# A kernel of one decoder layer: the left operands of the first feed-forward's deferred products are stored whole and split when they are fetched

## The chip, the cores and the metric

The kernel runs on one core of one Trainium2 chip. The core has engines with instruction queues of their own, each worked off in order: TensorE (PE; its weight loads are listed as PEld), VectorE (DVE), ScalarE (ACT), GpSimd (POOL), and SyncE (SP), which here issues all DMAs. The metric is the device time of one execution in microseconds (us); less is better.

## The reference

One layer of a sequence of 1024 tokens with width 1024: a half-step feed-forward, a mixer (a short convolution beside a state-space model), a second half-step feed-forward and a last norm. The change touches the two feed-forwards only.

```python
def swiglu(h, w_gate, w_up, w_down):
    return (jax.nn.silu(h @ w_gate) * (h @ w_up)) @ w_down
...
h = modulate(rms_norm(x, ffn1_norm[l]), sh1, sc1)
x = x + 0.5 * g1[:, None, :] * swiglu(h, ffn1_w_gate[l], ffn1_w_up[l], ffn1_w_down[l])
```

D_FF is 2816. All is float32.

## The kernel before

**Products.** A float32 product is made of three matmuls. Each operand is split into a high part (ScalarE rounds it to `fp32r`, a CAST) and a low part (VectorE subtracts the high part from the whole); then high x high, high x low and low x high are added in PSUM (`mm3`, line 333). A split operand of 128 x 512 is a tile of two halves, 512 KB; the whole is 256 KB.

**Groups.** The 22 column tiles of D_FF are taken in 11 groups of two. With the two halves of the tokens a group's activations are a 2 x 2 block matrix: A11, A12, A21, A22, each 128 x 512. For groups 4 to 10 of the first feed-forward (`fa4` to `fa10`) and 1 to 10 of the second (`fb1` to `fb10`) the gate and up products are made with seven block products in place of eight (`seven`, line 575): TensorE fills the PSUM banks A, B, C, D, E of the gate side, then of the up side (`fa8gC`: group 8, gate side, bank C), and VectorE adds them up in `t`, `u` tiles (`fa8gt`, `fa8gu`, `fa8ut`, `fa8uu`). Groups 0 to 3 of the first feed-forward use plain products (`gate_up`, line 1157).

**Deferred down products.** The down products of groups 1 to 8 are made later, in two chunks of four groups, again with seven block products, so their left operands are seven sums and blocks: A11, S1, S2, S3, A12, A22, S4 (`keep_sums`, `keep_last`, lines 490 to 501). Those of groups 0, 9 and 10 stay plain (`LAST`, line 39) and need the four A blocks. `keep` (line 482) splits an operand as soon as it is there, in a tile of the pool `movA`, and SyncE stores the 512 KB of both parts in DRAM. `fetch` (line 650) reads them back when a left operand of the chunk ahead has been used up.

**Passes.** `down7` (line 655) works a chunk in two passes, each over a quarter of the output columns from both halves. A pass has seven steps in the order A11, S2, A12, S3, S1, A22, S4 (`SECOND`, line 573), each 8 x 3 matmuls into banks A, B, C of two outputs (`fad_0A`: bank A of output 0). So there are passes 1 and 2 (chunk 0) and 3 and 4 (chunk 1). In a chunk's second pass each step's operand is given up, and SyncE fetches the next chunk's into the tiles that become free: `then(left)`. The operands of chunk 0 are fetched in the same way on the up side of group 10. The names of fetched tiles are `fa1lA`, `fa1lS` and so on: group 1, operand A.. or S... Behind pass 4 the last parts follow (`fald`, groups 0, 9, 10).

**Weights.** They come in `raw` tiles of 1 MB (two buffers), and one step of a pass needs one split weight tile `w` in a ring of three; `Weights.pump` (line 182) splits the next when a ring slot becomes free. A pass needs two raw tiles (`in_ds`), seven weight tiles with two halves, one from each raw tile; GpSimd makes four of the sums from the raw tiles (lines 164 to 175). The two raw tiles of the next pass can be loaded when the last weight tile of this one has been split.

**What sets the order.** The program is written in the order above, and side work (the state-space matrices, the modulation vectors `wm`) is let in by a count of matmuls (`Clock`). A scheduler then puts each engine's instructions in a row of its own, by the time at which it believes each can start and by the tiles that are free; in that row they run in order, so an instruction that waits holds all behind it.

Of the kernel before, what the change touches and what calls it, by code (L numbers as in the profile page):

```python
# [13 lines left out]
F32 = mybir.dt.float32  # L14
# [3 lines left out]
ALU = mybir.AluOpType  # L18
# [3 lines left out]
P = 128  # L22
D = 1024
S = 1024
HALF = 512
# [206 lines left out]
def hymba_layer(ctx: ExitStack, tc, x_d, wm1_d, wmod_d, gu1_d, gs1_d, ds1_d, wl1_d, win_d, wout_d, glu_d, gu2_d, gs2_d, wd2_d, ds2_d, wl2_d, cols_d, cond_d, lam_d, bc_d, out_d):  # L232
# [257 lines left out]
    def keep_sums(kept, a11, a21, a22, name):  # L490

        V.tensor_tensor(out=a22[:], in0=a21[:], in1=a22[:], op=ALU.add)
        keep(kept, "S1", a22, name)
        V.tensor_tensor(out=a21[:], in0=a11[:], in1=a21[:], op=ALU.subtract)
        keep(kept, "S3", a21, name)
        V.tensor_tensor(out=a22[:], in0=a22[:], in1=a11[:], op=ALU.subtract)
        keep(kept, "S2", a22, name)

    def keep_last(kept, a12, s2, name):
        V.tensor_tensor(out=a12[:], in0=a12[:], in1=s2[:], op=ALU.subtract)  # L500
        keep(kept, "S4", a12, name)

    def gu_keep(fi, h, pg, pu, afs, kept, name):
        t = t2k(f"{name}{fi}_{h}")
        A.activation(t[:], pg[:], AF.Silu)
        V.tensor_tensor(out=t[:], in0=t[:], in1=pu[:], op=ALU.mult)
        keep(kept, f"A{h + 1}{fi + 1}", t, name)
        afs[fi, h] = t
        if len(afs) == 4 and "S1" in kept:
            keep_sums(kept, afs[0, 0], afs[0, 1], afs[1, 1], name)  # L510
            keep_last(kept, afs[1, 0], afs[1, 1], name)
# [63 lines left out]
    def seven(name, between, place=1, kept=None, then=None):  # L575
# [4 lines left out]
        for side in "gu":  # L580
# [5 lines left out]
            def out(h, fi, t):  # L586
                nm = f"{name}_{fi}_{h}"
                if side == "g":
                    A.activation(t[:], t[:], AF.Silu)
                    gate_[h, fi] = t  # L590
                else:
                    V.tensor_tensor(out=t[:], in0=t[:], in1=gate_[h, fi][:], op=ALU.mult)
                    if kept is None:
                        a_tiles[fi, h] = split_act(t[:], nm + "a")
                    else:
                        keep(kept, f"A{h + 1}{fi + 1}", t, name)

            for n, (left, b) in enumerate(SEVEN):
# [26 lines left out]
                elif n == 4:  # L625
                    t = gate_[0, 0]
                    V.tensor_tensor(out=t[:], in0=t[:], in1=bank["A"][:], op=ALU.mult)
                    if kept is None:
# [1038 lines left out]
```

## Time and profile before

| what | us |
|---|---|
| median of 3 runs (1743.46 to 1748.77) | 1745.43 |
| the profiled execution, whole | 1741.48 |
| its span, first to last instruction | 1739.7 |
| groups of the first feed-forward | 50 to 501 |
| passes 1 to 4 | 501, 539, 582, 620, to 660 |
| last parts and the next norm | 660 to 730 |
| mixer | 730 to 1050 |
| second feed-forward: groups, passes | 1150 to 1510, 1510 to 1700 |

How to read the rows that follow: in a view by stage, each engine's busy time stands with its count of instructions, then the granted clock of TensorE (1.00 is full), the busy share of the DMA engines and their rate. In a view of time, a row has its start, its length, engine, line, operation and tiles, and in brackets the idle time of that engine ahead of it with what ended it. Nearly all instructions carry line 107, that of the helper which issues them, so one goes by the tiles' names; numbers of buffers are left out of them. In a view of waits, the three numbers are the total, the count and the longest. In a view of DMA issues, the last number is the median time from issue to landing.

### The profile page before, as it was taken

The page shows a single profiled execution, that of the slowest core. Times are in us where ns is not written, and L with a number is a line of the kernel's source. Part 1 is how long each engine was busy: PE and PEld are TensorE (multiplying, and loading weights), DVE is VectorE, ACT ScalarE, POOL GpSimd, SP SyncE. Part 2 cuts the span into 40 slices and gives each one's busy share as a digit, 9 for nine tenths or more (in the row PEclk, how much of TensorE's full clock was granted, in tenths as well). Part 3 has the DMA queues.
Part 4 walks back from the last instruction along what each step waited for, and adds up shares of the span by engine and source line. Part 5 has one row for each costly group of instructions (what it writes and reads, how often), then busy time and mean ns, then how long its engine had stood idle before and what let it go on. Part 6 is the DMA issues. An engine that isn't in the chain of part 4 may idle for free.

```text
span 1739.7 us, 20839 instructions
## 1 busy us (share of the span) xinstructions
PE 1672.0 (96%) x7532; PEld 1375.3 (79%) x7532; DVE 1291.1 (74%) x2261; ACT 573.3 (33%) x944; POOL 352.8 (20%) x241
## 2 busy tenths in 40 slices
PE   4999999999999999999999999999999999999996
PEld 3788888787887878887877778778888888888886
DVE  7999999998656787644657977967776666576656
ACT  4233334344332222331114424424444433322221
POOL 0000132222422221100000021123223323333211
PEclk9999999999999999999999999999999999999998
DMA  8245644555787877234654450114344334659212
GB/s 322 84 145 197 220 158 167 179 201 173 286 307 275 321 259 270 73 86 147 209 152 152 134 181 25 49 49 157 144 175 166 133 138 152 249 235 379 104 49 97
DMA packets 101338, 304.56 MB, mean 175 GB/s; under 512 B 19313, under 2 KB 34929, under 8 KB 90098
## 3 DMA queue, kind: packets, MB, share of 16 engines
q1 hardware_dynamic: 101234, 303.22, 49.0%
q8 instruction: 59, 0.97, 0.2%
q14 instruction: 45, 0.37, 0.1%
HBM read 212.47 MB, written 86.51 MB: 172 GB/s over the span
## 4 chain that ended last, share of the span: by engine, by line
PE 64%; DVE 8%; DMA 3%; issue 1%; ACT 0%; POOL 0%; SPq 0%; DVEq 0%; ACTq 0%; POOLq 0%
PE wo L107 4%; PE fald L107 3%; PE fb10d L107 2%; PE u L107 2%; PE fbd_1B L107 2%; PE fbd_0B L107 2%; PE fad_1B L107 2%; DVE w L107 2%; PE fad_0B L107 2%; PE b L107 2%; DMA swz<-si 1%; DVE x L107 1%; PE fb0g L107 1%; PE fbd_1C L107 1%; PE fbd_0C L107 1%; PE fbd_1A L107 1%
## 5 line engine op out<-in xcount | busy, mean ns | idle before, releaser
L107 ACT CAST w<-raw 128x512 fp32r<-128x512 f32 (+1 forms) x358 | 235.9, 689 | 459.1 <-issue 70.1
L107 DVE TENSOR_TENSOR w<-raw,w 128x512 fp32r<-128x512 f32 (+1 forms) x358 | 300.9, 860 | 100.8 <-ACT w L107 99.9
L164 POOL TENSOR_TENSOR sums<-raw 128x512 f32<-128x512 f32 x50 | 73.8, 1476 | 452.9 <-DMA raw<-in_gs 271.0
L173 POOL TENSOR_TENSOR raw<-sums,raw 128x512 f32<-128x512 f32 x50 | 78.4, 1568 | 367.3 <-DVE w L107 353.7
L107 DVE CUSTOM_DVE_ANT_0 wm<-wm,cact 128x1024 f32<-128x1024 f32 x56 | 77.7, 1396 | 22.6 <-DMA wm<-in_wmod 22.6
L175 POOL TENSOR_TENSOR raw<-raw 128x512 f32<-128x512 f32 x50 | 77.1, 1542 | 79.1 <-DVE w L107 79.1
L165 POOL TENSOR_TENSOR raw<-raw 128x512 f32<-128x512 f32 x50 | 77.3, 1547 | 3.1
L366 POOL TENSOR_TENSOR n3aq<-n3aq,n3aq 128x512 f32<-128x512 f32 x5 | 7.4, 1474 | 279.1 <-ACT n3aq L107 278.9
L107 DVE TENSOR_TENSOR w<-sums,w 128x512 fp32r<-128x512 f32 x50 | 56.7, 1147 | 5.4 <-ACT w L107 4.8
L107 PE MATMUL p<-h,w 128*128 128x512 f32 x192 | 49.6, 421 | 8.1 <-DVE h L107 5.3
L107 PEld LDWEIGHTS p<-h,w 128*128 128x128 f32 x192 | 39.1, 205 | 18.6 <-DVE h L107 6.5
L107 PE MATMUL wo<-oa,w 128*128 128x512 f32 x192 | 45.6, 392 | 2.1 <-ACT w L107 1.4
L107 PE MATMUL v<-h,w 128*128 128x512 f32 x192 | 46.8, 395 | 0.0
L107 PE MATMUL c<-h,w 128*128 128x512 f32 x192 | 46.6, 394 | 0.0
L107 PE MATMUL b<-h,w 128*128 128x512 f32 x192 | 45.6, 393 | 0.0
L107 PE MATMUL wo<-ob,w 128*128 128x512 f32 x192 | 45.5, 392 | 0.0
L107 PE MATMUL u<-h,w 128*128 128x512 f32 x192 | 44.7, 391 | 0.2 <-DVE h L107 0.2
L107 PEld LDWEIGHTS wo<-oa,w 128*128 128x128 f32 x192 | 35.8, 188 | 10.2 <-ACT w L107 1.8
L107 PEld LDWEIGHTS u<-h,w 128*128 128x128 f32 x192 | 35.7, 188 | 8.3 <-DVE h L107 0.6
L107 PEld LDWEIGHTS wo<-ob,w 128*128 128x128 f32 x192 | 35.7, 188 | 7.7 <-DVE ob L107 0.4
L107 PEld LDWEIGHTS b<-h,w 128*128 128x128 f32 x192 | 35.5, 188 | 7.2
L107 PEld LDWEIGHTS c<-h,w 128*128 128x128 f32 x192 | 35.4, 188 | 7.0
(1566 smaller groups left out, 4028.4 us busy)
## 6 DMA issues: line engine op xcount, KB each, us to landing
raw<-in_gs SPq DMA_DIRECT2D x34, 1024.0 KB, 5.5
wm<-in_wmod SPq DMA_DIRECT2D x56, 512.0 KB, 5.8
raw<-in_ds SPq DMA_DIRECT2D x16, 1024.0 KB, 6.8
raw<-in_gu SPq DMA_DIRECT2D x10, 1024.0 KB, 7.1
mw<-in_wm SPq DMA_DIRECT2D x8, 1024.0 KB, 12.4
x<-in_x SPq DMA_DIRECT2D x16, 512.0 KB, 8.3
raw<-in_win SPq DMA_DIRECT2D x8, 1024.0 KB, 5.6
raw<-in_wl SPq DMA_DIRECT2D x5, 1024.0 KB, 6.6
```

Of the source, the lines that this page charges most:

```text
L107: r = getattr(self.engine, name)(*args, **kw)
L164: self.G.tensor_tensor(out=f, in0=r[2], in1=r[1], op=ALU.subtract)
L165: self.G.tensor_tensor(out=r[1], in0=r[1], in1=r[0], op=ALU.subtract)
L173: self.G.tensor_tensor(out=r, in0=s["t3"], in1=r, op=ALU.add)
L175: self.G.tensor_tensor(out=r, in0=self.chunk(j, 3), in1=r, op=ALU.subtract)
L366: nc.gpsimd.tensor_tensor(out=a, in0=a, in1=sq[:, :n], op=ALU.add)
```

## The change

In the first feed-forward an operand is no longer split when it is made. VectorE writes the product or sum straight into one half of a plain float32 tile, and when both halves are there, SyncE stores the tile: two operands in one store of 512 KB. The pairs are X (A22, A11), Y (A21, A12), Z (S1, S3) and W (S2, S4), so groups 1 to 8 store A21 too, which nobody fetches. `fetch` reads one operand, 256 KB, into the low half of its tile; then ScalarE casts the high part from it, and VectorE subtracts in place. In the second feed-forward the operands are split when they are made, as before; but the list of what is stored now holds all eight, so A21 is split and stored there as well.

```diff
-    def keep(kept, left, src, name):
-
-        if left in kept:
-            t = mov(f"{name}{left}")
-            A.copy(t[:, 0, :], src[:])
-            V.tensor_tensor(out=t[:, 1, :], in0=src[:], in1=t[:, 0, :].bitcast(F32), op=ALU.subtract)
-            SP.dma_start(kept[left][:], t[:].bitcast(F32))
+    HALVES = dict(A22=("X", 0), A11=("X", 1), A21=("Y", 0), A12=("Y", 1), S1=("Z", 0), S3=("Z", 1), S2=("W", 0), S4=("W", 1))
+    class Kept:
+        def __init__(self, name, sums, split):
+            self.sums, self.split = sums, split
+            names = [left for left in HALVES if sums or left[0] == "A"] if split else "XYZW" if sums else "XY"
+            self.dram = {t: scratch.tile([P, 2, HALF], F32, name=f"{name}{t}") for t in names}
+            self.there, self.tiles = {}, {}
+        def place(self, left, name, home):
+            if self.split:
+                self.tiles[left] = home
+                return home
+            t, i = HALVES[left]
+            if t not in self.tiles:
+                self.tiles[t] = mov(f"{name}{t}", dtype=F32)
+            return self.tiles[t][:, i, :]
+        def done(self, left, name):
+            if self.split:
+                if left in self.dram:
+                    t = mov(f"{name}{left}")
+                    A.copy(t[:, 0, :], self.tiles[left])
+                    V.tensor_tensor(out=t[:, 1, :], in0=self.tiles[left], in1=t[:, 0, :].bitcast(F32), op=ALU.subtract)
+                    SP.dma_start(self.dram[left][:], t[:].bitcast(F32))
+                return
+            t, i = HALVES[left]
+            self.there.setdefault(t, set()).add(i)
+            if len(self.there[t]) == 2:
+                SP.dma_start(self.dram[t][:], self.tiles[t][:])
...
+    def keep(kept, left, a, b, op, name, home=None):
+        V.tensor_tensor(out=kept.place(left, name, home), in0=a, in1=b, op=op)
+        kept.done(left, name)
...
     def fetch(kept, left, where, name):
         t = mov(f"{name}{left}", where)
-        SP.dma_start(t[:].bitcast(F32), kept[left][:])
-        return t[:, 0, :], t[:, 1, :]
+        hi, lo = t[:, 0, :], t[:, 1, :]
+        if kept.split:
+            SP.dma_start(t[:].bitcast(F32), kept.dram[left][:])
+            return hi, lo
+        whole_ = lo.bitcast(F32)
+        SP.dma_start(whole_, kept.stored(left))
+        A.copy(hi, whole_)
+        V.tensor_tensor(out=lo, in0=whole_, in1=hi.bitcast(F32), op=ALU.subtract)
+        return hi, lo
...
-    kept = {g: kept_for(g, g not in LAST[1]) for g in range(1, NGRP - 1)}
+    kept = {g: kept_for(g, g not in LAST[1], True) for g in range(1, NGRP - 1)}
```

Three places show how the rows move; numbers behind a name's last underscore only tell buffers apart. The first is SyncE's row in pass 1, where group 10's last store, the last fetches of chunk 0 and the raw weights of pass 2 (`raw24`, `raw25`) meet. Before:

```order
L107 DMA fa1lS4_4619<-kept1S4_545 128x1024
L107 DMA kept10A12_600<-fa10A12_4610 128x1024
L107 DMA fa2lS4_4621<-kept2S4_552 128x1024
L107 DMA fa3lS4_4623<-kept3S4_559 128x1024
L107 DMA fa4lS4_4625<-kept4S4_566 128x1024
L107 DMA raw24_4765<-in_ds1 128x2048
L107 DMA raw25_4797<-in_ds1 128x2048
L107 DMA fa5lA11_4915<-kept5A11_567 128x1024
```

and with the change:

```order
L107 DMA fa1lS4_4441<-kept1W_540 128x512
L107 DMA kept10Y_572<-fa10Y_4403 128x1024
L107 DMA fa2lS4_4445<-kept2W_544 128x512
L107 DMA fa3lS4_4449<-kept3W_548 128x512
L107 DMA fa4lS4_4453<-kept4W_552 128x512
L107 DMA fa5lA11_4745<-kept5X_553 128x512
L107 DMA fa6lA11_4749<-kept6X_557 128x512
L107 DMA fa7lA11_4753<-kept7X_561 128x512
L107 DMA fa8lA11_4757<-kept8X_565 128x512
L107 DMA raw24_4595<-in_ds1 128x2048
L107 DMA raw25_4627<-in_ds1 128x2048
```

The store now takes a plain product, the fetches are half as long, and the first fetches of chunk 1 have moved ahead of the raw weights.

The second is VectorE's row on the way to the weight tile of pass 1's third step (`w67`). Before, two splits of group 10's kept operands and group 10's last sums stood there:

```order
L107 TENSOR_TENSOR fa10A22_4525<-fa10ut1_4434,fa10A22_4525 128x512
L107 TENSOR_TENSOR fa10A11_4550<-fa10gc11_4385,fa10A11_4550 128x512
L107 TENSOR_TENSOR w66_4554<-raw23_4441,w66_4554 128x512
L107 TENSOR_TENSOR fa10uu3_4521<-fa10uu3_4521,fa10uE_4569 128x512
L107 TENSOR_TENSOR fa10uu3_4521<-fa10uu3_4521,fa10gu3_4363 128x512
L107 TENSOR_TENSOR fa10uu2_4485<-fa10uu2_4485,fa10uC_4451 128x512
L107 TENSOR_TENSOR w67_4614<-raw22_4333,w67_4614 128x512
L107 TENSOR_TENSOR fa10uu2_4485<-fa10uu2_4485,fa10gu2_4348 128x512
L107 TENSOR_TENSOR w67_4614<-raw23_4441,w67_4614 128x512
```

and with the change (the last part of that stretch):

```order
L107 TENSOR_TENSOR w66_4366<-raw23_4227,w66_4366 128x512
L107 TENSOR_TENSOR fa1lA12_4373<-fa1lA12_4373 128x512
L107 TENSOR_TENSOR fa10uu3_4331<-fa10uu3_4331,fa10uE_4389 128x512
L107 TENSOR_TENSOR fa2lA12_4377<-fa2lA12_4377 128x512
L107 TENSOR_TENSOR fa10Y_4403<-fa10uu3_4331,fa10gu3_4149 128x512
L107 TENSOR_TENSOR fa3lA12_4381<-fa3lA12_4381 128x512
L107 TENSOR_TENSOR fa4lA12_4385<-fa4lA12_4385 128x512
L107 TENSOR_TENSOR fa10uu2_4287<-fa10uu2_4287,fa10uC_4245 128x512
L107 TENSOR_TENSOR w67_4436<-raw22_4119,w67_4436 128x512
L107 TENSOR_TENSOR fa10Y_4403<-fa10uu2_4287,fa10gu2_4134 128x512
L107 TENSOR_TENSOR fa1lA22_4405<-fa1lA22_4405 128x512
L107 TENSOR_TENSOR fa2lA22_4409<-fa2lA22_4409 128x512
```

Fetched splits (`fa1lA12` and so on, in place) stand between the sums; in the whole stretch from group 10's A11 product to the second half of `w67` there are 11 of them (one of S2, four each of S3 and A12, two of A22), and the two kept splits are gone.

The third is VectorE's row at the first weight tiles of pass 2 (`w72`, `w73`, `w74`). Before, the second half of `w72` (from `raw25`) stood behind the first halves of the two tiles that follow:

```order
L107 TENSOR_TENSOR w72_4805<-raw24_4765,w72_4805 128x512
L107 TENSOR_TENSOR fad0_0_1u2_4690<-fad0_0_1u2_4690,fad0_0_1C_4782 128x512
L107 SCALAR_TENSOR_TENSOR x2_0_4286<-fad0_0_1u2_4690,gate_93,x2_0_4286 128x512
L107 TENSOR_TENSOR w73_4840<-raw24_4765,w73_4840 128x512
L107 TENSOR_TENSOR w74_4875<-raw24_4765,w74_4875 128x512
L107 TENSOR_TENSOR w72_4805<-raw25_4797,w72_4805 128x512
```

and with the change:

```order
L107 TENSOR_TENSOR w72_4635<-raw24_4595,w72_4635 128x512
L107 TENSOR_TENSOR fad0_0_0t1_4470<-fad0_0_0t1_4470,fad0_0_0B_4492 128x512
L107 SCALAR_TENSOR_TENSOR x0_1_4074<-fad0_0_0t1_4470,gate_93,x0_1_4074 128x512
L107 TENSOR_TENSOR w72_4635<-raw25_4627,w72_4635 128x512
L107 TENSOR_TENSOR fad0_0_1t1_4485<-fad0_0_1t1_4485,fad0_0_1B_4507 128x512
L107 TENSOR_TENSOR w73_4670<-raw24_4595,w73_4670 128x512
```

The second half now follows the first with two operations between. ScalarE's row has the same order of halves, and at the first tile of pass 4 both rows move in the same way.

More of the change, by code (lines that the diff above doesn't have):

```diff
@@ L639, in seven @@
                     out(0, 1, u2)
-                    if side == "u" and kept is not None and "S1" in kept:
-                        keep_last(kept, u2, t1, name)
+                    if side == "u" and kept is not None and kept.sums:
+                        keep_last(kept, name)
                 if q % 2:
```

56 lines of the change are left out of this document (29 added, 27 removed).

## The prediction

> **What bounds the kernel now.** I read the page's totals first, then the busy time by stage, then TensorE's waits, and then the order of time around the longest of them.
>
> ```profile
> span 1739.7 us, 20839 instructions
> ...
> PE 1672.0 (96%) x7532; PEld 1375.3 (79%) x7532; DVE 1291.1 (74%) x2261; ACT 573.3 (33%) x944; POOL 352.8 (20%) x241
> ```
>
> TensorE (PE) is in work for 96% of the span, so only its gaps can be won. The next table is the view of busy time by stage, cut where the first feed-forward's stages begin and end: its groups, the four passes of `down7`, the last parts, and for comparison the groups and passes of the second feed-forward.
>
> ```profile
> core 0: us, PE busy (x) PEld busy (x) DVE busy (x) ACT busy (x) POOL busy (x), PEclk, DMA share, GB/s
> ...
> 50.00:500.90 450.90, 447.32 (x2008) 366.66 (x2007) 404.65 (x864) 171.97 (x292) 99.58 (x63) 1.00 0.53 185
> 500.90:539.00 38.10, 38.10 (x170) 31.55 (x169) 23.90 (x35) 8.45 (x15) 3.91 (x3) 1.00 0.94 342
> 539.00:582.00 43.00, 40.46 (x169) 32.39 (x168) 29.13 (x35) 10.21 (x18) 17.62 (x12) 0.96 0.77 295
> 582.00:620.10 38.10, 38.10 (x169) 31.54 (x169) 29.03 (x43) 8.96 (x16) 10.44 (x9) 1.00 0.78 299
> 620.10:660.20 40.10, 38.38 (x169) 31.45 (x168) 33.73 (x51) 9.20 (x15) 6.16 (x4) 1.00 0.72 260
> 660.20:730.00 69.80, 69.80 (x317) 58.03 (x317) 47.70 (x72) 19.29 (x26) 13.54 (x8) 1.00 0.43 156
> 1150.00:1510.00 360.00, 360.00 (x1590) 298.10 (x1589) 243.62 (x355) 142.15 (x251) 109.61 (x76) 1.00 0.42 153
> 1510.00:1700.00 190.00, 190.00 (x840) 157.34 (x839) 121.17 (x153) 48.28 (x84) 53.53 (x37) 1.00 0.51 198
> ```
>
> The reader is to see three things. A pass lasts 38.10 us when nothing stops TensorE (first and third); the second lasts 43.00 and the fourth 40.10, so 4.9 and 2.0 us are lost. In the groups VectorE (DVE) is busy for 404.65 of 450.90 us, 90%, and TensorE loses 450.90 - 447.32 = 3.6 us. The second feed-forward loses nothing (360.00 of 360.00, 190.00 of 190.00) with VectorE at 68% and 64%. TensorE's waits between 150 and 730 us name the same places:
>
> ```profile
> PE fad_0A L107 <- DVE w L107: 3.9, 3, 1.9
> PE fa8gC L107 <- DVE fa8gt L107: 2.2, 1, 2.2
> PE fa6gC L107 <- DVE fa6gt L107: 0.9, 1, 0.9
> ...
> PE fa7gC L107 <- DVE fa7gt L107: 0.3, 1, 0.3
> PE fa4gC L107 <- DVE fa4gt L107: 0.2, 1, 0.2
> ```
>
> The four waits of groups 4, 6, 7 and 8 are 3.6 us, all for VectorE's sum of the second product at a group's start. All that the change can take away is therefore 3.6 + 4.9 + 2.0 = **10.5 us**.
>
> Why the second pass starts late is read from three queues: SyncE's issues (SPq), then ScalarE (ACT), then TensorE.
>
> ```profile
> 517.24 0.63 SPq L107 DMA_DIRECT2D fa1lS<-kept1S  x1
> 525.42 0.32 SPq L107 DMA_DIRECT2D kept10A<-fa10A  x1
> 527.59 1.00 SPq L107 DMA_DIRECT2D raw<-in_ds  x2
> ...
> 536.27 0.62 ACT L107 CAST w<-raw 128x512 fp32r<-128x512 f32 x1 [11.77 <-DMA raw<-in_ds]
> ...
> 545.87 0.52 PE L107 MATMUL fad_0A<-fa3lA,w 128*128 128x512 f32 x1 [1.86 <-DVE w L107]
> ```
>
> SyncE stands from 517.9 to 525.4 before the last store of group 10, which waits for a split; behind it come three fetches and then the weights of pass 2 (`raw` from `in_ds`, issued at 527.6), which ScalarE waits 11.8 us for. From there the sums and splits of the weights run too late for TensorE. In pass 4 the weights were issued in time, and the second half of the first weight tile is split behind a half of the next tile, at 622.02:
>
> ```profile
> 606.96 0.93 SPq L107 DMA_DIRECT2D raw<-in_ds  x2
> ...
> 622.02 1.75 DVE L107 TENSOR_TENSOR w<-raw,w 128x512 fp32r<-128x512 f32 x1
> ...
> 623.82 0.50 PE L107 MATMUL fad_0A<-fa7lA,w 128*128 128x512 f32 x1 [1.72 <-DVE w L107]
> ```
>
> **The change, part by part.** *Price of a split.* One ScalarE cast and one VectorE subtraction, and here the store as well:
>
> ```profile
> L107 ACT CAST fa1S<-fa x4: 621/622/622, 134.1 to 138.0; 128x512 fp32r<-128x512 f32 x4
> L107 DVE TENSOR_TENSOR fa1S<-fa,fa1S x4: 683/690/692, 134.7 to 139.1; 128x512 fp32r<-128x512 f32 x4
> ```
>
> The first feed-forward has 8 groups of seven operands and 3 of four: 68 splits, 68 x 0.69 = 46.9 us of VectorE and 68 x 0.62 = 42.2 us of ScalarE. None vanishes; all move to where an operand is fetched.
>
> *Groups.* 66 of them lie ahead of 500.9 us (the last two of group 10 came later), so VectorE falls there by 66 x 0.69 = 45.5, less the 11 fetched splits that now stand in group 10 (7.6): 404.65 - 37.9 = 366.7 of 447.3 us, 82%. That is between the 90% that loses 3.6 us and the 68% of the second feed-forward that loses nothing. The waits sit where a group's last four splits meet the next group's first sums, and these splits go. I take all 3.6 us: **-3.6**.
>
> *Stores and loads.* 68 stores of 512 KB become 38 (four in each of 8 groups, two in 3); 68 loads of 512 KB become 68 of 256 KB. That is 15.7 MB stored and 17.8 MB loaded less. In pass 1 the DMA share is 0.94, so transfers there wait for each other; each fetch halves. A 256 KB load in this stretch is not shown alone; bounds: 3.7 us (the quickest median of a 512 KB load) and 12.3 us (the slowest).
>
> ```profile
> fa5lS<-kept5S SPq DMA_DIRECT2D x4, 512.0 KB, 3.7
> ...
> fa7lA<-kept7A SPq DMA_DIRECT2D x3, 512.0 KB, 12.3
> ```
>
> I take 4, near the lower end, since with half the bytes the queue is shorter.
>
> *Weights of pass 2.* The store that held SyncE no longer waits for a split but for the product itself, which VectorE now writes before 512. The weights then wait only for their buffer, that is for the last weight tile of pass 1. Its split follows the release of a ring slot at the end of step 4 (about 522.6), so they go out at 525 if VectorE is not late, and land without fetches beside them. Besides, the two halves of the first tile now stand one behind the other in VectorE's row (front rows, `w72`), not three tiles apart. This ends the 4.9 us: **-4.9**. In pass 4 the first tile's halves are together as well: **-2.0** at most.
>
> *What the passes get.* Of the 68 splits, 11 stand ahead of VectorE's last product of `fa10uA`; 57 fall into the passes, less the two late splits of group 10: 55 x 0.69 = 38.0 us. VectorE before: 23.90 + 29.13 + 29.03 + 33.73 = 115.8. After: 153.8 us, against 4 x 38.1 = 152.4 of TensorE. **VectorE gets as much work as TensorE.** It may run late by some us without harm, as a fetched operand is due about 32 us after its buffer came free (six of seven steps of 5.44), but a weight tile or a bank sum is due within two steps.
>
> Pass 1 is the tight place. The first row is the split of the second half of `w67`, the tile of the pass's third step; the second is TensorE's start of its third step:
>
> ```profile
> 505.48 0.68 DVE L107 TENSOR_TENSOR w<-raw,w 128x512 fp32r<-128x512 f32 x1
> ...
> 511.76 0.84 PE L107 MATMUL fad_0B<-fa1lS,w 128*128 128x512 f32 x3
> ```
>
> Between the last product of `fa10uA` and that half stand 11 fetched splits now and two kept ones less: 506.2 + 9 x 0.69 = 512.4, and 1 to 2 us more for the seven splits ahead that find little idle time and for a collision with GpSimd. It is due at 511.8 + 1.4 + 0.5 = 513.6. So 513.4 to 514.4 against 513.6: a stall of 0 to 1, and another as small at the bank sums of the next step. I put **+1.5** for pass 1, **+2.0** for pass 4 (it has the highest load, 33.73 before plus some 8 splits, so what it wins I take as lost again), and **+0.6** for the two between.
>
> *Collisions.* A VectorE operation that meets GpSimd takes longer, as here, where 0.69 became 1.78:
>
> ```profile
> 538.08 1.78 DVE L107 TENSOR_TENSOR w<-raw,w 128x512 fp32r<-128x512 f32 x1
> ...
> 537.68 1.62 POOL L165 TENSOR_TENSOR raw<-raw 128x512 f32<-128x512 f32 x1
> ```
>
> The sums above hold the collisions of before, not new ones. The Trainium skill, page "SBUF — State Buffer", section "Who interferes with whom", says that a VectorE instruction with two SBUF inputs contends with a GpSimd instruction that reads SBUF, and that the loser blocks fully; the split subtraction has two such inputs, the bank sums have one from PSUM. The row agrees. By that rule more of GpSimd's 28 instructions in the passes would cost a VectorE operation about 1.1 us each, which is the third rival below.
>
> *Second feed-forward.* Although it keeps its splits, its list of stored operands now holds A21 too: eight more splits and stores, 8 x 0.69 = 5.5 us of VectorE over 360 us at 68%. TensorE's full 360.00 hides them; exposed they would cost up to 5.5.
>
> **Sum.** -3.6 - 4.9 - 2.0 + 1.5 + 2.0 + 0.6 = **-6.4** us on the profiled execution's 1741.48: 1735.1. The median of the runs is 1745.43, 3.95 above it; the same step from there gives **1739.0**.
>
> **Rivals.**
> - *All stalls go and none comes.* -10.5: **1734.9**. For it: VectorE may be late within the rings, and the passes of the second feed-forward run clean. Against it: 153.8 us of work in 152.4.
> - *The fetch casts hold ScalarE's row.* They stand ahead of weight casts, and each waits for its load; at landings near the upper end, 12 us, a weight tile that is due two steps after its slot came free (10.9 us) is late by 1 to 2 us, in four or five steps of passes 1 and 2. The passes win nothing, the groups 3.6 or less: **1742 to 1746**.
> - *VectorE is the bound of the passes, through GpSimd (slower).* If nearly each of the 28 GpSimd instructions stops an operation for a further 0.6 to 1.1 us, VectorE has 153.8 + 17 to 31 us, say 172 against the 159.3 that the passes last now (38.1 + 43.0 + 38.1 + 40.1 us): +13 - 3.6, **about 1754**. It decides from 5.5 us of new collisions on (no gain in the passes) and makes the kernel slower from 9.1. For it: a row without gaps meets every GpSimd instruction. Against it: many sums of GpSimd wait for VectorE's own splits and so do not overlap.
> - *The change does not do what it says:* the A21 splits of the second feed-forward come into the open: -6.4 + 5.5, **1744.5**.
>
> **How the numbers follow.** A measurement of this kernel can tell about 0.3% (5.2 us) from no change. Chances: forecast 0.42, all stalls gone 0.16, casts held 0.28, collisions 0.10, A21 exposed 0.04. Faster by over 0.3% (below 1740.2): most of the first case and the second, 0.55. Within: 0.35. Slower: 0.10. The range takes the second case with a little spread of the median below it, and the held casts with 2 us above: **1733.5 to 1748**; collisions and some tails are left out.
>
> **What would show it.** Right: no wait of `fa8gC` for `fa8gt`; no `kept10` store that holds SyncE; weights of pass 2 out before 527; VectorE busy over 36 us in each pass; pass 2 under 40 us. Wrong: a pass over 42 us with TensorE waiting for `w` or for a bank sum; VectorE's mean for a fetched split well above 0.8 us (collisions); ScalarE waiting for `fa..l` loads ahead of a weight cast; any wait of TensorE between 1150 and 1700.

## The result and the profile after

| | before | changed |
|---|---|---|
| median (range) of 22 runs each, us | 1745.34 (1742.04 to 1749.39) | 1740.72 (1735.52 to 1746.36) |
| ratio, 95% interval | | 0.9975 (0.9967 to 0.9983) |
| the profiled execution, us | 1741.48 | 1735.52 |
| forecast | | 1739.0, range 1733.5 to 1748 |

The median fell by 4.6 us (0.27%), which lies just within the 0.3% taken as no change; 6.4 us had been forecast. The first lines are those of the changed kernel's page:

```profile
span 1733.7 us, 20843 instructions
...
PE 1669.1 (96%) x7532; PEld 1373.3 (79%) x7532; DVE 1287.4 (74%) x2269; ACT 579.0 (33%) x952; POOL 350.5 (20%) x241
```

The busy time by stage, cut at the changed kernel's own marks (groups, passes 1 to 4, then groups and passes of the second feed-forward):

```profile
86.00:495.86 409.86, 409.30 (x1847) 336.19 (x1846) 327.38 (x675) 133.86 (x224) 93.46 (x62) 1.00 0.46 157
495.86:535.04 39.18, 38.44 (x169) 31.32 (x168) 35.81 (x53) 17.97 (x33) 9.20 (x6) 1.00 0.54 182
535.04:573.12 38.08, 38.08 (x169) 31.53 (x168) 34.69 (x49) 19.28 (x35) 12.39 (x9) 1.00 0.65 219
573.12:613.88 40.76, 38.92 (x169) 31.30 (x168) 40.31 (x62) 12.34 (x24) 9.32 (x7) 1.00 0.63 208
613.88:654.43 40.55, 39.00 (x170) 31.22 (x168) 36.53 (x54) 15.98 (x27) 10.30 (x7) 1.00 0.55 193
...
1150.00:1510.00 360.00, 360.00 (x1590) 298.10 (x1589) 249.07 (x362) 145.12 (x258) 107.94 (x75) 1.00 0.44 167
1510.00:1700.00 190.00, 190.00 (x840) 157.34 (x839) 120.57 (x153) 49.16 (x85) 56.15 (x40) 1.00 0.48 187
```

VectorE falls in the groups and rises to 35 to 40 us in passes of 38 to 41; the DMA share of pass 1 falls from 0.94 to 0.54. Pass 2 is clean. Pass 3, which was clean before, now loses 2.7 us, and VectorE is busy there for 40.31 of 40.76 us. The waits of TensorE between 150 and 730 us:

```profile
PE fad_0A L107 <- DVE w L107: 1.9, 2, 1.1
PE fad_0B L107 <- ACT w L107: 1.3, 1, 1.3
PE fad_0B L107 <- DVE w L107: 0.9, 2, 0.5
PE fa10uC L107 <- DVE fa10ut L107: 0.6, 1, 0.6
```

No group from 4 to 8 waits any more, group 10 does for 0.6 us; in place of those and of pass 2's waits stand five short ones in passes 1, 3 and 4, put down to weight tiles. SyncE's last store of group 10 and the weights of pass 2, which it issued at 525.42 and 527.59 before the change:

```profile
507.64 0.32 SPq L107 DMA_DIRECT2D kept10Y<-fa10Y  x1
...
524.52 0.92 SPq L107 DMA_DIRECT2D raw<-in_ds  x2
```

A second profile of the same kernel (told below) allows a table by stretch, from the start of one to the start of the next:

| stretch, us | before | changed | changed, second profile | forecast of the change |
|---|---|---|---|---|
| up to group 1 | 86.5 | 85.3 | 85.5 | 0 |
| groups 1 to 10 | 414.4 | 410.6 | 410.4 | -3.6 |
| pass 1 | 38.1 | 39.2 | 40.3 | +1.5 |
| pass 2 | 43.1 | 38.1 | 38.1 | -4.9, and a part of +0.6 |
| pass 3 | 38.1 | 40.8 | 40.4 | a part of +0.6 |
| pass 4 | 40.1 | 40.6 | 42.5 | -2.0 + 2.0 |
| the rest | 1079.5 | 1079.3 | 1082.3 | 0 |

The 0.9 to 1.2 us ahead of group 1 are not from the change: four kernels below with the same groups (experiments 1, 3, 5 and 6) show 86.1 to 86.8 there, like the kernel before. Single executions differ by some us: the two profiled ones of the changed kernel took 1735.52 and 1741.26, that is 6.0 and 0.2 us less than the profiled one of before, on both sides of the 4.6 of the medians.

### The profile page after: what moved, and what is told of

The parts are those of the page before. It is cut to its first block, busy times and chain, and to the rows that moved or that the text cites. A ratio compares the mean times of both kernels' runs of the same rounds, so it can differ in the third digit from the quotient of the medians.

```text
span 1733.7 us, 20843 instructions
## 1 busy us (share of the span) xinstructions
PE 1669.1 (96%) x7532; PEld 1373.3 (79%) x7532; DVE 1287.4 (74%) x2269; ACT 579.0 (33%) x952; POOL 350.5 (20%) x241
## 4 chain that ended last, share of the span: by engine, by line
PE 48%; DVE 6%; DMA 3%; issue 1%; ACT 0%; SPq 0%; DVEq 0%; ACTq 0%
PE wo L107 4%; PE fb10d L107 2%; PE u L107 2%; PE fbd_1B L107 2%; PE fbd_0B L107 2%; PE v L107 2%; PE b L107 2%; DMA swz<-si 1%; PE fb0g L107 1%; PE fbd_1C L107 1%; PE fbd_0C L107 1%; PE fbd_1A L107 1%; PE fbd_0A L107 1%; DVE x L107 1%; PE gl L107 1%; PE yy L107 1%
## 5 line engine op out<-in xcount | busy, mean ns | idle before, releaser
L107 PEld LDWEIGHTS p<-h,w 128*128 128x128 f32 x192 | 38.5, 202 | 18.0 <-DVE h L107 6.4
L107 DVE TENSOR_TENSOR w<-sums,w 128x512 fp32r<-128x512 f32 x50 | 50.9, 1031 | 2.2 <-ACT w L107 1.8
L107 ACT CAST w<-sums 128x512 fp32r<-128x512 f32 x50 | 30.3, 620 | 32.5 <-PE fa7gE L107 2.2
```

The costliest lines, as they stand in the source:

```text
L107: r = getattr(self.engine, name)(*args, **kw)
```

## Experiments

Each kernel was compared with the kernel before on the same chip; differences below are between medians, and lengths of passes are those of one profiled execution each. "Fetched splits" are those that the change puts into the passes.

**1. Group 10 alone split when made.** The store that was to hold SyncE is a split one again.

```diff
-    kept = {g: kept_for(g, g not in LAST[0]) for g in range(NGRP)}
+    kept = {g: kept_for(g, g not in LAST[0], g == NGRP - 1) for g in range(NGRP)}
```

> One part undone: group 10 alone splits its four operands when they are made and stores them in four stores; groups 0 to 9 stay whole. In VectorE's row the two halves of pass 2's first weight tile stay together, as in the changed kernel. Theory A (the splits of groups 1 to 8 made the group waits; pass 2 was late because a store of group 10 waits for its split and holds SyncE, with the raw weights behind it): no waits of fa4gC to fa8gC, the raw weights of pass 2 are issued 26 us or more after the pass 1 began (28.6 in the changed kernel, 26.7 before, where pass 1 was shorter), pass 2 lasts 41 to 44 us; the whole is -1 to +1 us against before. Theory B (pass 2 was late because the halves stood three tiles apart): pass 2 lasts 38 to 39 us, the whole is -4 to -6 us.

Measured: 1739.78 against 1744.42, **-4.6 us** (ratio 0.9961 to 0.9987). By stage, passes 1 and 2:

```profile
496.32:534.45 38.13, 38.13 (x170) 31.45 (x168) 37.78 (x58) 21.43 (x38) 16.03 (x6) 1.00 0.65 221
534.45:572.53 38.08, 38.08 (x170) 31.53 (x168) 35.77 (x50) 19.81 (x35) 13.76 (x10) 1.00 0.65 225
```

Pass 2 stays clean, so theory A falls in this form: that group 10's operands are split does not by itself make pass 2 late. The figures of theory B came true, but the weights also land earlier here than before the change (6.3 and 3.9 us ahead of pass 2, before 2.8 and 0.4), so this run does not part the two theories. The table on pass 2 in the next section takes that up. The last two of its stores went out at 508.3 and 513.0, that is 12.0 and 16.7 us into the pass; before the change it was 13.7 and 24.5. Another thing shows: pass 1 loses nothing here, with 37.78 us of VectorE, more than the 35.81 of the changed kernel, which loses 1.1. So in pass 1 it is not the load alone. The order of VectorE's row does not settle it either: experiment 8 has the same order there, and its pass 1 lasted 39.2 us. The cause is left open.

**2. The converse: groups 1 to 8 split, 0, 9 and 10 whole.** First with A21 split and stored too, then without.

```diff
+    kept = {g: kept_for(g, g not in LAST[0], g not in LAST[0]) for g in range(NGRP)}
...
+            names = [left for left in HALVES if (left != "A21" if sums else left[0] == "A")] if split else "XYZW" if sums else "XY"
```

> The converse: groups 1 to 8 split when the operands are made and are fetched with 512 KB, groups 0, 9 and 10 are whole. The two halves of pass 2's first weight tile stand apart again, with a half of the next tile between. Theory A: the waits of fa4gC, fa6gC, fa7gC, fa8gC stay (3 to 4 us), pass 2 lasts 38.1 to 39.5 us, passes 1 and 3 have no new stall (38.1), pass 4 about 40; the whole is -4 to -5 us against before. Theory B: pass 2 lasts 41 to 43 us and the whole is 0 to -2. Theory C (the gain is that of fewer bytes moved): with the fetches at 512 KB pass 2 stays at 41 to 43 and the whole at 0 to -1.

> As the earlier run with groups 1 to 8 split when made and groups 0, 9 and 10 whole, but A21 of groups 1 to 8 is neither split nor stored, as before the change; that run had eight splits more in the groups, and its group waits were 7.6 us in place of 3.6. Theory A (the group waits are VectorE's splits): group waits 3 to 4.5 us, pass 2 38.1 to 39.5, the four passes together 154 to 156 us, the whole -3 to -5 us against before. Rival (the waits come from something else that this split brings, as the whole tiles of the three groups): group waits 7 us or more, the whole +1 to +3.

Measured: +2.2 us with A21 (1746.63 against 1744.42, ratio 1.0004 to 1.0032), **-5.5** without (1739.84 against 1745.30, 0.9960 to 0.9983). TensorE's waits in the groups, with A21:

```profile
PE fa8gC L107 <- DVE fa8gt L107: 2.7, 1, 2.7
PE fa5gC L107 <- DVE fa5gt L107: 2.2, 1, 2.2
PE fa7gC L107 <- DVE fa7gt L107: 1.7, 1, 1.7
PE fa6uC L107 <- DVE fa6ut L107: 0.8, 1, 0.8
```

and without it:

```profile
PE fa8gC L107 <- DVE fa8gt L107: 2.3, 1, 2.3
PE fa6gC L107 <- DVE fa6gt L107: 1.1, 1, 1.1
...
PE fa7gC L107 <- DVE fa7gt L107: 0.3, 1, 0.3
```

Three doses of splits in the groups give three sums of waits of groups 4 to 8: none of groups 1 to 8 (the changed kernel), no wait; seven of each, 3.7 us; eight of each, 7.6 us. So VectorE's splits make the group waits. The first of the two runs missed its expectation because the second feed-forward's list with A21 had come along. In the second, pass 2 lasts 38.9 us although each fetch again moves 512 KB and the halves stand apart; the four passes together last 154.2 us, 4.4 less than in the changed kernel.

**3. Fetches of 512 KB.**

```diff
-        SP.dma_start(whole_, kept.stored(left))
+        SP.dma_start(t[:].bitcast(F32), kept.dram[HALVES[left][0]][:])
```

> The changed kernel, but each fetch loads the whole tile of two operands, 512 KB, and uses the half that lands in the low place; for operands in the other half the wrong one is used. 17.8 MB more are read, as before the change. The two halves of pass 2's first weight tile stand apart in VectorE's row, as before. Theory A: neither matters much; group waits gone, pass 2 38 to 39.5 us, the whole -3 to -5.5 us against before. Theory B: pass 2 loses 2 us or more. Theory C (bytes): loads land 4 us later, casts hold ScalarE, the passes lose 3 us or more against the changed kernel and the whole is 0 to -2.

Measured: **-3.9 us** (1740.50 against 1744.42, 0.9965 to 0.9984); the changed kernel's median was 1740.72. Pass 2 lasts 39.5 us, and the weights for it land in 4.9 and 6.8 us. Theory C falls: with as many bytes fetched as before, nearly all of the gain is there.

**4. Two stores of group 10 moved off SyncE, in the kernel before.** First the fourth store alone (A12), then the third and the fourth; ScalarE issues them. The edit shown is the second.

```diff
-            SP.dma_start(kept[left][:], t[:].bitcast(F32))
+            (A if name == "fa10" and left in ("A21", "A12") else SP).dma_start(kept[left][:], t[:].bitcast(F32))
```

> The kernel before with one store moved: the last store of group 10 (kept10 from fa10A, operand A12) is issued by ScalarE, behind its own cast, and no longer by SyncE. All splits, tiles and bytes stay; the two halves of pass 2's first weight tile stay three tiles apart. Theory A, as the first runs leave it (the store held SyncE, so three fetches of 512 KB went out in one burst ahead of the raw weights, which were issued late and landed in 8.6 and 10.5 us in place of 4.9 and 6.8): the raw weights of pass 2 go out 13 to 14.5 us ahead of the pass (11.4 before), land in under 7.5 us, pass 2 lasts 38.5 to 39.8 us, the group waits stay, the whole is -3 to -4.5 us against before. Theory B (the halves that stand apart make the loss): pass 2 stays at 42 or more and the whole within 1 us of before.

> The kernel before with two stores moved: the third and the fourth store of group 10 (operands A21 and A12) are issued by ScalarE behind their casts and no longer by SyncE; the run with the fourth alone moved left SyncE standing for the third until 14 us into pass 1, and the weights of pass 2 landed in 9.5 and 11.5 us behind a full queue. All splits and bytes stay, and the halves of pass 2's first weight tile stay apart. Theory D (the two stores hold SyncE, the fetches behind them bunch up, and the raw weights land behind that bunch): the A22 and S4 fetches go out earlier, the raw weights land in under 7.5 us, pass 2 lasts 38.5 to 39.8 us, the whole is -2.5 to -4.5 us against before. Rival (512 KB stores and loads fill the queue whatever the order): landings stay above 8 us, pass 2 lasts 41 us or more, the whole within 1.5 us of before.

Measured: the fourth alone -2.5 us (1742.78 against 1745.30, 0.9977 to 0.9997), both **-6.2** (1740.02 against 1746.20, 0.9948 to 0.9975). SyncE with the fourth alone moved, in pass 1 (from 502.9):

```profile
507.62 0.52 SPq L107 DMA_DIRECT2D fa4lA<-kept4A  x1
516.52 0.32 SPq L107 DMA_DIRECT2D kept10A<-fa10A  x1
...
526.24 0.94 SPq L107 DMA_DIRECT2D raw<-in_ds  x2
```

It still stands from 508.1 to 516.5 before the third store; then eight fetches of 512 KB go out within 7 us, and ScalarE has the first of the weights only at 535.8, 9.5 us after the issue:

```profile
535.78 0.62 ACT L107 CAST w<-raw 128x512 fp32r<-128x512 f32 x1 [9.29 <-DMA raw<-in_ds]
541.56 2.18 ACT L107 CAST w<-raw 128x512 fp32r<-128x512 f32 x4 [5.16 <-POOL raw L173]
```

The second row is four casts in one; going by the order of halves before the change (`w73`, `w74`, then `w72`), the third is the second half of the first weight tile. It stands behind halves of the next two tiles, which wait for a sum of GpSimd, and so starts at 542.6, 1.7 us after pass 2 has begun (540.94); TensorE waits for it until 543.27. Pass 2 lasted 44.1 us in place of the 38.5 to 39.8 expected. That execution was the slowest of its ten, so the median, not this length, says what the fourth store alone is worth; it, too, fell short of the 3 to 4.5 us expected. With both moved, by stage:

```profile
502.55:540.64 38.09, 38.09 (x170) 31.52 (x168) 25.76 (x36) 9.35 (x17) 6.66 (x6) 1.00 0.99 386
540.64:579.60 38.96, 38.85 (x170) 31.30 (x168) 26.22 (x34) 9.21 (x17) 14.45 (x10) 1.00 0.83 314
579.60:617.68 38.08, 38.08 (x170) 31.53 (x168) 32.47 (x47) 8.96 (x16) 12.19 (x9) 1.00 0.79 299
617.68:655.79 38.11, 38.11 (x169) 31.45 (x168) 29.73 (x44) 9.20 (x15) 6.15 (x4) 1.00 0.71 251
```

All four passes are all but clean: 153.2 us in place of 159.4, with every operand split when it is made and every byte moved as before. Pass 2 gains 4.1 us; the 2.0 of pass 4 had not been expected and are not explained. So theory D holds for the cause, the two waiting stores; its landing time was missed (8.1 and 8.3 us, under 7.5 expected), and it did not need to be that short. The Trainium skill, page "DMA: Bandwidth & Descriptors", section "Issuing engines are not separate DMA queues", says that DMAs issued by different engines share the same 16 DMA engines, and that issuing on several saves only the time to initiate them, which is usually small. On the first half the trace shows only that pass 1's DMA share, counted over those 16 engines, is 0.99 with both stores moved. For a store that waits for its data the second half does not hold here: in the kernel before SyncE issued nothing from 505.8 to 514.5 and from 517.9 to 525.4, each time up to one of these stores, and moving both was worth 6.2 us.

**5. Most of the fetched splits taken away.**

```diff
-        V.tensor_tensor(out=lo, in0=whole_, in1=hi.bitcast(F32), op=ALU.subtract)
+        V.tensor_tensor(out=lo[:, :32], in0=whole_[:, :32], in1=hi[:, :32].bitcast(F32), op=ALU.subtract)
```

> The changed kernel, but VectorE forms the low part of each fetched operand for 32 of its 512 columns only, so most of the low parts of the deferred products are not formed: 0.69 us a piece becomes some 0.1, some 33 us of VectorE's work leave the four passes. Casts and loads stay. Theory A (the new stalls of the passes are VectorE's load): passes 1 to 4 last 38.1 to 38.8 us each, the whole is 3.5 to 5 us below the changed kernel, -8 to -10 against before. Rival (ScalarE's casts that wait for loads make the stalls): pass 3 stays above 40 us, the whole stays within 1.5 us of the changed kernel.

Measured: **-11.7 us** (1732.72 against 1744.42, 0.9917 to 0.9948), 8 below the changed kernel. Passes 1 to 3 last 38.08 us each, pass 4 39.2:

```profile
496.63:534.71 38.08, 38.08 (x169) 31.54 (x168) 28.49 (x53) 17.90 (x33) 12.07 (x8) 1.00 0.55 191
...
572.79:610.87 38.08, 38.08 (x169) 31.54 (x168) 35.17 (x63) 13.32 (x24) 7.44 (x7) 1.00 0.62 217
```

ScalarE's casts are all there (17.90 us of ScalarE in pass 1, 17.97 in the changed kernel), so they do not hold the row; VectorE's subtractions make the new stalls. This is what they cost: 5.1 us of the passes in the first profile, 7.8 in the second.

**6. The modulation vectors started later.** Their products (`wm`) are VectorE work of 1.21 us each that has stood in passes 3 and 4 all along.

```diff
-    clock.side.append(side2(mod_mov, (SC2, SH2, G2)))
-    down7("fad1", lefts[1], 0, fetch_last)
+    def mods_late(left):
+        if left == "S4":
+            clock.period = 6
+            clock.side.append(side2(mod_mov, (SC2, SH2, G2)))
+    down7("fad1", lefts[1], 0, fetch_last, mods_late)
```

> The changed kernel, but the modulation vectors (24 operations of VectorE of 1.22 us, ten of them in pass 3) start only when pass 3 has ended, one every 6 ticks in place of 8. Theory A (pass 3 loses 2.7 us because fetched splits and modulation vectors together fill VectorE: 40.3 of 40.8 us): pass 3 lasts 38.1 to 39 us, and the vectors cost 0 to 3 us more in pass 4 and the last parts; the whole 0 to -2.5 us against the changed kernel. Rival (ScalarE's casts of fetched operands hold the weight casts): pass 3 stays at 40 us or more and the whole is not below the changed kernel.

Measured: **-7.7 us** (1738.46 against 1746.20, 0.9933 to 0.9967); the changed kernel, run beside it, had 1741.74. By stage, passes 3 and 4:

```profile
574.99:613.87 38.88, 38.32 (x169) 31.45 (x168) 36.30 (x52) 13.65 (x25) 11.51 (x9) 1.00 0.33 119
613.87:651.95 38.08, 38.08 (x169) 31.53 (x168) 36.14 (x57) 14.08 (x23) 5.78 (x4) 1.00 0.67 231
```

Three of the vectors are left in pass 3 in place of ten, and passes 3 and 4 together last 77.0 us in place of 81.3. VectorE's row in pass 3 of the changed kernel, where they meet the fetched splits:

```profile
586.76 0.68 DVE L107 TENSOR_TENSOR fa8lS<-fa8lS 128x512 fp32r<-128x512 f32 x1
587.36 1.22 DVE L107 CUSTOM_DVE_ANT_0 wm<-wm,cact 128x1024 f32<-128x1024 f32 x1
...
588.50 1.29 DVE L107 TENSOR_TENSOR w<-sums,w 128x512 fp32r<-128x512 f32 x2
589.71 1.21 DVE L107 CUSTOM_DVE_ANT_0 wm<-wm,cact 128x1024 f32<-128x1024 f32 x1
...
590.86 0.68 DVE L107 TENSOR_TENSOR fad_0u<-fad_0t,fad_0B 128x512 f32<-128x512 f32 x1
```

and TensorE behind it:

```profile
591.68 0.93 PE L107 MATMUL fad_0B<-fa5lS,w 128*128 128x512 f32 x3 [1.30 <-ACT w L107]
```

The view names a cast as what ended this wait, since one ended at about that time; but the bank sum ended at 591.54, and it has to have read bank B before the step S3, whose first matmul this is, adds to that bank. So this stall, too, is VectorE's.

**7. Fewer fetched splits.** One run splits groups 0, 9 and 10 when made; the other splits all A operands when made and keeps only the sums S1 to S4 whole.

```diff
+    kept = {g: kept_for(g, g not in LAST[0], g in LAST[0]) for g in range(NGRP)}
```
```diff
...
+        def splits(self, left):
+            return self.split or left[0] == "A"
...
```

> The changed kernel with groups 0, 9 and 10 split when made, as before the change; groups 1 to 8 whole. 56 fetched splits in place of 68, all twelve taken from pass 4 and its surroundings, 8.3 us of VectorE. Theory A (VectorE's load makes the new stalls): no group waits, passes 1 and 2 as in the run with group 10 alone split (38.1 each), passes 3 and 4 together 77 to 79.5 us in place of 81.3; the whole -6 to -8 us against before. Rival (ScalarE's casts of chunk 1, which stay, make them): passes 3 and 4 together 81 us or more, the whole -4 to -5.

> A mixture in the first feed-forward: the A operands of all groups are split when made and stored split, as before the change (A21 of groups 1 to 8 is not stored), and the sums S1 to S4 are stored whole in pairs and split when fetched. 32 fetched splits in place of 68; the four splits that stood at a group's end stay away from it. Theory A: VectorE at about 85% in the groups loses 0 to 1 us there; the passes lose 1 to 3 us in all in place of the 6 of the changed kernel's profile; the whole is -6 to -9 us against before, below the changed kernel. Rival (any VectorE load above 82% in the groups brings the waits back): group waits 2 us or more, the whole -2 to -4.

Measured: **-7.3 us** (1738.03, 0.9942 to 0.9974) and **-7.1** (1738.22, 0.9938 to 0.9974) against 1745.30. With the last groups split, pass 1 lost nothing (38.18), but passes 3 and 4 still took 81.3 us, as the rival said. The passes took 157.6 us in all, 1.0 less than in the first profile of the changed kernel; the rest of the gain in the medians is not explained. With the mixture, one group wait came back (fa8gC, 1.7 us), and the passes lasted 157.1 us.

**8. Some fetched splits on GpSimd**, on top of the first kernel of 7.

```diff
+        late = name[:3] in ("fa5", "fa6", "fa7", "fa8") and left in ("S3", "S1", "A22", "S4")
+        (nc.gpsimd if late else V).tensor_tensor(out=lo, in0=whole_, in1=hi.bitcast(F32), op=ALU.subtract)
```

> The run with groups 0, 9 and 10 split when made, and of chunk 1's fetched operands S3, S1, A22 and S4 of groups 5 to 8 are subtracted by GpSimd: 16 subtractions of 0.69 us leave VectorE in passes 2 to 4 and cost GpSimd about 1.3 to 1.7 us each there. Theory A (VectorE's load makes the stalls of passes 3 and 4): those two together 78 to 80 us in place of 81.3, the whole 1 to 3 us below that run (-8 to -10 against before). Rival (GpSimd stops VectorE and delays the weight sums of its own row): passes 2 to 4 together 1 us or more longer than in that run (119.4), the whole -2 to -6.

Measured: +0.2 us (1746.38 against 1746.20, 0.9990 to 1.0017), 7.5 us worse than without it: the rival. Pass 3 lasted 48.4 us, with one wait of 7.7 us for a bank sum of VectorE. GpSimd's row ahead of the end of that wait (599.37):

```profile
588.60 2.27 POOL L695 TENSOR_TENSOR fa5lS<-fa5lS 128x512 fp32r<-128x512 f32 x1
590.83 2.25 POOL L695 TENSOR_TENSOR fa6lS<-fa6lS 128x512 fp32r<-128x512 f32 x1
```

and VectorE's, in which the sum that TensorE waits for stands just before the last of these rows:

```profile
587.41 2.31 DVE L107 CUSTOM_DVE_ANT_0 wm<-wm,cact 128x1024 f32<-128x1024 f32 x1
...
589.65 2.30 DVE L107 CUSTOM_DVE_ANT_0 wm<-wm,cact 128x1024 f32<-128x1024 f32 x1
...
599.15 1.21 DVE L107 CUSTOM_DVE_ANT_0 wm<-wm,cact 128x1024 f32<-128x1024 f32 x1
```

**9. The changed kernel once more.**

> The changed kernel once more, for a second profile and for runs on one chip with the other three. If the profiled gain of 6.0 us against the 4.6 of the medians is chance outside the change: the four passes together again 157.5 to 159.5 us with the same waits, groups without waits of fa4gC to fa8gC, and the difference to the first profile lies in the stretch up to the first group (a lower granted clock there) and in the mixer. If the stalls themselves vary: the passes together differ by 2 us or more from 158.6.

Measured: 1741.74 against 1746.20 (-4.5 us, 0.9964 to 0.9984), as in the first comparison. The passes of this execution, 1 to 4:

```profile
495.95:536.24 40.29, 38.73 (x169) 31.30 (x168) 36.76 (x55) 19.61 (x36) 8.97 (x6) 1.00 0.53 177
536.24:574.32 38.08, 38.08 (x169) 31.53 (x168) 35.71 (x50) 19.91 (x36) 13.35 (x10) 1.00 0.63 218
574.32:614.71 40.39, 38.68 (x170) 31.30 (x168) 39.60 (x61) 11.91 (x22) 8.75 (x6) 1.00 0.62 211
614.71:657.19 42.48, 40.27 (x170) 32.56 (x168) 40.15 (x57) 15.90 (x27) 9.80 (x7) 0.96 0.55 196
```

161.2 us in place of 158.6 for the same rows: the stalls themselves vary from one execution to the next, in passes 1 and 4. This is the second of the two cases, and it fits the wider range of the changed kernel's 22 runs (10.8 us, before 7.4), though the ten runs of this second comparison span 3.7 us only. The 3 us that this execution lost behind the passes were not followed up.

## Why the prediction was right or wrong

The median came out 1.7 us above the forecast and inside its range; that the gain would be over 0.3%, given the larger chance, did not come true by a little. The gain is 1.8 us short of the 6.4 forecast, about as much as passes 1, 3 and 4 took beyond their share of the sum in the first profile (4.2 us, 2.1 forecast). Step by step:

- *Groups, -3.6:* right, in mechanism and size. The profiles gain 3.8 and 4.0 us there, and experiment 2 gives the waits back in proportion to the splits.
- *Pass 2, -4.9:* the size is right (-5.0 in both profiles). The prediction named two causes, the last store of group 10, which "no longer waits for a split but for the product itself", and the halves of the first weight tile, which now stand one behind the other. Both are at work. The table has the time from the landing of each of the two raw tiles to the start of pass 2, from one profile each:

| kernel | halves | landed ahead of pass 2, us | pass 2, us |
|---|---|---|---|
| before | apart | 2.8, 0.4 | 43.1 |
| 4, fourth store moved | apart | 5.2, 2.6 | 44.1 |
| 4, both stores moved | apart | 6.2, 3.8 | 39.0 |
| 7, the mixture | apart | 6.7, 4.2 | 38.5 |
| 3, and both of 2 | apart | 8.2 to 9.2, 5.7 to 6.7 | 38.9 to 39.5 |
| changed, second profile | together | 5.4, 2.9 | 38.1 |
| changed | together | 5.6, 3.2 | 38.1 |

  The remaining kernels have the halves together, the first raw tile 5.6 us ahead or more, and pass 2 at 38.1. With the halves apart the loss all but goes once the tiles land 6.2 and 3.8 us ahead; this is the part of the late weights. But the changed kernel's land only 5.4 to 5.6 and 2.9 to 3.2 us ahead, hardly earlier than those of experiment 4 with one store moved, which lost 6.0 us. The second half of its first tile is cast 2.9 us ahead of pass 2 (536.24) in the second profile, as soon as the second raw tile has landed, and 1.7 us after its start in experiment 4:

```profile
533.34 0.62 ACT L107 CAST w<-raw 128x512 fp32r<-128x512 f32 x1 [1.74 <-DMA raw<-in_ds]
```

  So at the changed kernel's lead the order of the halves decides, as far as two single profiles show it; how much each of the two causes gave there stays open, since no run has the halves together with weights as late as before. On the store the prediction was right in that it goes out right behind the product now (507.64), but experiment 1 splits group 10 again, in another order of the rows, and pass 2 stays clean.

  That the weights went out at 524.5, as forecast (525), is luck. The 525 was reckoned from a pass 1 that starts at 500.9, so 24.1 us into it; it started at 495.9, and they went out 28.7 us into it, later than the 26.7 of before. Without most of the fetched splits it is 23.4 (experiment 5), so the load of VectorE, which holds up the last weight tile of pass 1, takes some 5 us here. The weights are earlier all the same because they land in 4.9 and 6.7 us in place of 8.6 and 10.5, "without fetches beside them", as the prediction said.
- *Passes 1, 3 and 4:* here the sum was mis-sized. Pass 1 was given +1.5 and took +1.1 and +2.2. The "+0.6 for the two between" is +2.7 and +2.3, all of it in pass 3; pass 4, taken as neither won nor lost, took +0.4 and +2.4. The step that failed is the count of VectorE's work: it set the splits beside the load of before as if that stayed where it was. The modulation vectors of pass 3, before and after:

```profile
L107 DVE CUSTOM_DVE_ANT_0 wm<-wm,cact x7: 1216/1223/1229, 599.2 to 612.8; 128x1024 f32<-128x1024 f32 x7
```

```profile
L107 DVE CUSTOM_DVE_ANT_0 wm<-wm,cact x10: 1209/1215/1218, 587.4 to 610.0; 128x1024 f32<-128x1024 f32 x10
```

  Ten stand there in place of seven, from 14 us into the pass in place of 17. Counted the forecast's way, pass 3 would have 29.03 us and nine fetched splits of 0.69, that is 35.2; it has 40.31, and three vectors of 1.22 are 3.7 of the difference. Experiment 6 moves seven of them out and gets 4.3 us of passes 3 and 4 back. In pass 1 the place was right: the wait of 0.74 us stands in the third step, for its weight tile. The row that the prediction gives for that step's start before the change is of the step S3 (bank B), which TensorE's row there had ahead of A12; the time is still that of the third step.
- *The load of VectorE, 153.8 us forecast:* 147.3 in the first profile, though 57 of the 68 fetched splits did fall into the passes, as counted. That the passes would take about 4.1 us of new stalls was the right view; experiment 5 shows 5 to 8.
- *Fetch loads at 4 us:* a little short, without harm. The medians of the 256 KB loads in the view of DMA issues run from 2.5 us (`fa10lA<-kept10Y`) to 8.4 (`fa6lS<-kept6Z`); most lie between 4 and 6.
- *Rivals:* the casts did not hold ScalarE's row (experiment 5). New collisions with GpSimd were few: the 68 fetched splits took 0.76 us in the mean, seven of them over 1 us. Of the four of group 7's S operands, three took about 0.69 us and one 1.77:

```profile
L107 DVE TENSOR_TENSOR fa7lS<-fa7lS x4: 681/690/1772, 552.7 to 586.2; 128x512 fp32r<-128x512 f32 x4
```

  That rival becomes real when GpSimd is given more (experiment 8). The A21 splits of the second feed-forward are hidden: VectorE has 5.5 us more there, TensorE 360.00 of 360.00; where VectorE is near its limit, the same eight splits cost 4 us (experiment 2).
- *What would show it:* no wait of `fa8gC`, weights out at 524.5 and pass 2 under 40 us came as said, the second by luck. VectorE over 36 us in each pass did not: it has 35.81 and 34.69 in passes 1 and 2. SyncE is still held: `kept10Y` went out at 507.64, but ahead of the time at which it matters. A pass over 42 us, one of the signs of being wrong, did show in the second profile.

So the accounts are: the change wins 3.8 to 4.0 us in the groups and loses 4.2 in the first profile and 6.9 in the second in passes 1, 3 and 4, so that by these two profiles moving the splits brings nothing by itself, or a loss. It is faster because pass 2's loss goes, and for that no operand has to be split elsewhere: moving two stores to another issuing engine wins 6.2 us without it. Other versions, too, gained more than the changed kernel's 4.5 to 4.6: the later modulation vectors (7.7), the last groups split when made (7.3), the mixture (7.1), groups 1 to 8 split without A21 (5.5). Their intervals overlap with each other; only that of the later vectors (0.9933 to 0.9967) hardly touches the changed kernel's (0.9964 to 0.9984). Putting the moved stores together with whole operands and later vectors was not tried.

## What to carry to other kernels

Work that is moved from a busy stage has to be set against the stage that receives it, with what else is queued there as it will then stand, not as it stood. A DMA that waits for its data holds all DMAs behind it on the issuing engine (here for 8.7 and 7.5 us), so a late transfer of weights is to be followed back through the queue to each store that waits, not only to the last. How late weights may land depends on the order in which the rows use them: in the profiles here, 5.4 us ahead was enough with the halves of a tile together, and 5.2 was not with them apart. Where one change does two things, do each of them alone before crediting the larger one.

## What had not been expected of the hardware

- *GpSimd and VectorE both slow down.* In experiment 8 a `wm` product takes 2.3 us beside GpSimd's subtraction and 1.21 alone, and the subtraction 2.25 us beside it and 1.29 at its shortest. The Trainium skill, page "SBUF — State Buffer", section "Who interferes with whom", has the one that issues second blocked until the first has finished. In the rows of experiment 8 a product and a subtraction go by every 2.2 us, which is not quite the 2.5 of one behind the other, so the rows agree in the main. Neither row has gaps there, and both engines pay: four products lost 4.3 us, four subtractions 3.8.
- *A pause of TensorE can cost more than its length.* In the kernel before, pass 2's waits are 2.5 us (3.9 + 0.3 us of `fad_0A` in the view of waits, less the 1.72 of pass 4), but the pass loses 4.9. The view by stage shows the rest as a lower granted clock behind the waits:

```profile
401.26:404.30 3.04, 3.04 (x13) 2.52 (x14) 3.04 (x4) 2.04 (x4) 1.68 (x1) 1.00 0.94 334
...
543.00:546.00 3.00, 1.09 (x4) 0.62 (x5) 3.00 (x4) 0.52 (x1) 2.37 (x2) 1.00 0.88 330
546.00:549.00 3.00, 3.00 (x8) 2.37 (x9) 1.50 (x1) 0.34 (x1) 2.55 (x2) 0.54 0.02 7
549.00:553.00 4.00, 4.00 (x17) 3.24 (x17) 2.69 (x4) 2.40 (x5) 1.30 (x1) 0.92 0.00 0
```

  From 543 on TensorE was busy for 1.09 of 3 us, and the clock of the next 3 us was 0.54, of the 4 after them 0.92: 3 x 0.46 + 4 x 0.08 = 1.7 of the 2.4 us. The single wait for `fa8gt`, 2.2 us, which ends where the first row begins, was followed by a clock of 1.00.
